# Hybrid decoder layer on one core: sums of weight blocks made by accumulating transfers, and the out-projection's operands fetched inside the last pair of products

## The chip, the cores and the metric

The kernel runs on one core of a Trainium2 chip. The metric is the device time of one execution in microseconds (us), from the runs of one measurement. The core's engines are PE (TensorE, matrix products), DVE (VectorE), ACT (ScalarE), POOL (GpSimd) and SP (SyncE, which here only issues transfers). "PEld" is PE's weight load, "PEclk" the clock that was granted to PE.

## The reference, cut to what matters

One layer (DEPTH = 1) of a decoder trunk, in float32, for 1024 positions of width 1024: an HGRN2 mixer with 8 heads of 128, then a squared-ReLU MLP.

```python
def _hgrn2_mixer(h, w_in, lower_bound, out_norm, w_out):
    proj = h @ w_in                              # 1024 x 4096
    q, f, i, g = jnp.split(proj, 4, axis=-1)
    ...                                          # log_f, k from f; qf = silu(q) / sqrt(128)
    o = _hgrn2_chunk_scan(heads(qf), heads(k), heads(i), heads(log_f))
    # S_t = diag(f_t) S_{t-1} + k_t v_t^T ; o_t = S_t^T q_t, for each head
    o = o * lax.rsqrt(jnp.mean(o * o, axis=-1, keepdims=True) + NORM_EPS)
    o = o.reshape(b, s, D_MODEL) * out_norm * jax.nn.silu(g)
    return o @ w_out

def reference(...):
    x = x + _hgrn2_mixer(_rmsnorm(x, norm_mix), ...)
    x = x + _squared_relu_mlp(_rmsnorm(x, norm_mlp), w1, w2)   # relu(h@w1)**2 @ w2
    return _rmsnorm(x, norm_final)
```

## The kernel before

**Products.** Each float32 operand is split in two parts of a shorter format: hi is a copy on ACT, lo the difference on DVE. A product is then three matmuls, hi·hi, hi·lo and lo·hi (`split_mm`, L208 to L210, 128x512 each).

**The projection h @ w_in** is cut into 16 pieces ("pairs", `pair`), n = 2h + j: for head h, j = 0 gives q and f, j = 1 gives v and g. The weights of piece n come as four blocks of 128x512, a, b, c, d: SP loads them in two transfers of 512 KB (`load_raw`, L144), a and c in one tile (named raw n 0), b and d in the other (raw n 1). The first two pieces are multiplied plainly. The other 14 use seven products of half-size blocks in place of eight, so they need sums of weight blocks: c+d is s1, a+c is s3, a+c+d is s2 and a+b+c+d is s4, each made in place in a raw block by DVE adds (`add`, L148), four adds for each n. `ensure` makes, in the order a, b, s1, s2, s3, s4, d, first the sums that a block needs and then its split (ACT at L168, DVE at L169) into one of eight slots m4 to m11, by the running number modulo 8. A slot is free again when PE has done the product eight jobs back. PE takes the blocks in the order a, b, s2, s1, s3, s4, d, twelve matmuls each; the blocks are asked for six jobs ahead.

**The scan.** Between a head's matmuls PE's stream has the scan units of an earlier head in it (`scan_units`), handed out one at a time by `pump` at a set spacing: small (L477), middle (L510, which needs qe, made by ACT at L499 and L503 and DVE at L504), leaf (L528), big (L558), kt (L573), vt (L584), kv (L596, which needs v, copied by ACT at L585), o, z and zt. The tables of level scores go by lv and Ac, the running products of the gates by f, q and k, and R and ht are sums of blocks of the normalised input and their splits.

**The output projection** (`proj_out`) multiplies z, the gated and normalised output of the scan, by w_out. z of heads 0 to 6 goes out to DRAM (zd, L641) and comes back in the layout wanted (iz, L700), w_out's blocks come by iw (L700), both are split (zh, wo: ACT at L689, DVE at L690) by `fetch`. In the program's text all fetches stand behind the last pair. The last head's scan units are pumped into the output projection. The MLP follows.

**Order of the work.** PE's order is the order of the text. At the start, up to the first two plain half pieces, ACT's, DVE's and POOL's are too. Behind that a planner sets the order on ACT, DVE, POOL and SP, by its own costs and the tiles' dependences; it may move a transfer or a split far ahead of where the text has it. Each engine then runs its list in that order, and waits at an instruction until its operands are ready.

Of the kernel before, what the change touches and what calls it, by code (L numbers as in the profile page):

```python
# [21 lines left out]
F32 = mybir.dt.float32  # L22
F32R = mybir.dt.float32r
U8 = mybir.dt.uint8
AF = mybir.ActivationFunctionType
ALU = mybir.AluOpType
# [3 lines left out]
P = 128  # L30
D = 1024
T = 1024
NH = 8
NC = T // P
# [14 lines left out]
def trunk(ctx: ExitStack, tc: tile.TileContext, x, gains, masks, gfin, w_in, w_out, w1, w2, out):  # L49
    nc = tc.nc  # L50
    pool = ctx.enter_context(tc.tile_pool(name="keep", bufs=1))
# [21 lines left out]
    def mslot(i, shape, name, dt=F32):  # L73
        return pool.tile(shape, dt, name=name, tag=f"m{i}")

    def hslot(half, kb, name):
        return pool.tile([P, 2, 512], F32R, name=name, tag=f"hT{half}{kb}")

    def dslot(i, shape, name, dt=F32):
        return dp.tile(shape, dt, name=name, tag=f"d{i}")  # L80
# [36 lines left out]
    def load_x(tb):  # L117
        nc.sync.dma_start(xs[tb], x[tb * P:(tb + 1) * P, :])
# [13 lines left out]
    PLAIN = 2  # L132
    ORDER = (("X", "a", "B11"), ("Z", "b", "B21"), ("X", "s2", "t2"), ("Y", "s1", "t1"),
             ("X", "s3", "t3"), ("Y", "s4", "B22"), ("X", "d", "t4"))
    jobs = [(n, m) for n in range(2 * NH) for m in ("abcd" if n < PLAIN else ("a", "b", "s1", "s2", "s3", "s4", "d"))]
    index = {j: i for i, j in enumerate(jobs)}
    raws = {}
    split = {}

    def load_raw(n):  # L140
        if n < 2 * NH:
            two = [mslot(2 * (n % 2) + i, [P, 2, 512], f"raw{n}{i}") for i in range(2)]
            for i in range(2):
                nc.sync.dma_start(two[i], w_in[n, i])  # L144
            raws[n] = {"a": two[0][:, 0], "c": two[0][:, 1], "b": two[1][:, 0], "d": two[1][:, 1]}

    def add(out_, a, b):
        nc.vector.tensor_tensor(out_, a, b, ALU.add)  # L148

    def ensure(count):  # L150

        while len(split) < min(count, len(jobs)):
            i = len(split)
            n, m = jobs[i]
            r = raws[n]
            if m == "s1":
                add(r["a"], r["a"], r["c"])
                add(r["c"], r["c"], r["d"])
            if m == "s2":
                add(r["c"], r["a"], r["d"])  # L160
            if m == "s4":
                add(r["c"], r["c"], r["b"])
            src = r[{"s1": "c", "s2": "c", "s4": "c", "s3": "a"}.get(m, m)]
            w = mslot(4 + i % 8, [P, 2, 512], f"w{n}{m}", F32R)
            step = P if i < 1 else 512
            for c in range(0, 512, step):
                o = slice(c, c + step)
                nc.scalar.activation(w[:, 0, o], src[:, o], AF.Copy)  # L168
                nc.vector.tensor_tensor(w[:, 1, o], src[:, o], w[:, 0, o].bitcast(F32), ALU.subtract)  # L169
            split[i] = w  # L170
            if m == "d":
                load_raw(n + 2)

# [71 lines left out]
    z_d = [dram.tile([P, T], F32, name=f"zd{h}") for h in range(NH - 1)]  # L245
    with tc.tile_pool(name="scan", bufs=1) as sp:
# [13 lines left out]
        lo = pool.tile([P, 8], F32, name="lbe")  # L260
# [105 lines left out]
        def f_bound(h, f):  # L366
            nc.vector.tensor_scalar(f, f, omlb[:, h:h + 1], lb[:, h:h + 1], op0=ALU.mult, op1=ALU.add)
# [38 lines left out]
        def pair(h, tl, j):  # L406

            n = 2 * h + j
            bank = {}
            for i, (b, m, src) in enumerate(ORDER):  # L410
                first = b not in bank
                if first:
                    bank[b] = psum.tile([P, 512], F32, name=f"p{b}{n}", tag="d")
                p_ = bank[b]
                w = weight(n, m)
                for kb in range(4):
                    c = slice(kb * P, (kb + 1) * P)
                    t = hc[src, kb]
                    split_mm(p_, w[:, 0, c], w[:, 1, c], t[:, 0], t[:, 1], first and kb == 0, kb == 3,
                             skip_group_check=True)  # L420
                    if kb == 1:
                        ensure(index[n, m] + AHEAD)
                    pump(650.0)
                if m in ("a", "s2", "s4", "b"):
                    name = "q" if j == 0 else "vT"
                    tiles(h, tl, name)
                    half = int(m in ("s2", "s4"))
                    dst = tl[name][:, HALF[half]]
                    if m in ("a", "s2"):
                        nc.scalar.activation(dst, p_, AF.Copy)  # L430
                    else:
                        add(dst, dst, p_)
                        if j == 0 and half:
                            q_part(h, tl, 0, tl["q"])
                elif m == "s1":
                    e = part(h, f"e{j}")
                    nc.scalar.activation(e, p_, AF.Copy)
                elif m == "s3":
                    add(e, e, p_)
                    (f_half, g_half)[j](h, tl, 1, e, -1.0)  # L440
                else:
                    (f_half, g_half)[j](h, tl, 0, p_, -1.0)
                    if j == 0:
                        f_bound(h, tl["f"])

        def prefixes(tl):

# [13 lines left out]
        def scan_units(h, tl):  # L461
# [60 lines left out]
            def leaf(m, i):  # L522
                def run():
                    ps = psum.tile([P, NC, LEAF], F32, name=f"lv{h}_{m}", tag="s")
                    for c in range(NC):
                        for b in range(P // LEAF):
                            s = slice(c * P + b * LEAF, c * P + (b + 1) * LEAF)
                            nc.tensor.matmul(ps[b * LEAF:(b + 1) * LEAF, c, :], k[:, s], q[:, s],  # L528
                                             start=True, stop=True)
                    carry(m)  # L530
                    nc.vector.copy_predicated(Ac, mk[:, i:i + 1, :].to_broadcast([P, NC, LEAF]), ps)  # L531
                    if m == LEAF // 2:
                        for b in range(P // LEAF):
                            r = slice(b * LEAF, (b + 1) * LEAF)
                            nc.scalar.activation(AT[r, :, r], Ac[r, :, :], AF.Copy)  # L535
                return run
# [93 lines left out]
            def zt():  # L630

                z = tl["sg"]
                for a in range(2):
# [7 lines left out]
                        nc.sync.dma_start(z_d[h][:, o], z[:, o])  # L641
                free("sg")

            return ([None] * (6 if h == 0 else 3) + [small, None, None] + [middle, None, leaf(16, 7)]
                    + [big(32), big(64), None, kt, ("values", h), vt, kv, None, o_unit, z_unit, None, zt])


        heads = {0: {}}
# [25 lines left out]
            pair(h, tl, 1)  # L674
            complete.add(("values", h))


        zh, wo = {}, {}
        items = [("z", half, h) for half in (0,) for h in range(NH - 1)] + [("w", 0, h) for h in range(NH)]
        items += [("z", 1, h) for h in range(NH - 1)] + [("w", 1, h) for h in range(NH)]  # L680
        item_no = [0]

        def place(what, half, h):
            if what == "z":
                return hslot(half, (h, (h + 4) % 8)[half], f"zh{half}{h}")
            return dslot((h, (8, 9, 10, 11, 0, 1, 2, 3)[h])[half], [P, 2, 512], f"wo{half}{h}", F32R)

        def split_value(t, src):
            nc.scalar.activation(t[:, 0], src, AF.Copy)  # L689
            nc.vector.tensor_tensor(t[:, 1], src, t[:, 0].bitcast(F32), ALU.subtract)  # L690

        def fetch(what, half, lo, hi):

            for h0 in range(lo, hi, 2):
                raw = mslot(item_no[0] % 4, [P, 2, 512], f"i{what}{half}{h0}")
                item_no[0] += 1
                for i in range(min(2, hi - h0)):
                    h = h0 + i
                    src = z_d[h][:, HALF[half]] if what == "z" else w_out[h * P:(h + 1) * P, HALF[half]]
                    nc.sync.dma_start(raw[:, i], src)  # L700
                for i in range(min(2, hi - h0)):
                    h = h0 + i
                    t = (zh if what == "z" else wo)[half, h] = place(what, half, h)
                    split_value(t, raw[:, i])

        xs = [mslot(4 + tb, [P, D], f"xr{tb}") for tb in range(NC)]

        def proj_out(tbs, dh, hs, after=None):

# [11 lines left out]

        o0 = slice(0, 512)
        A, B = range(NC // 2), range(NC // 2, NC)
        last = NH - 1
        fetch("z", 0, 0, last)
        fetch("w", 0, 0, last)
        for tb in range(NC):
            load_x(tb)
        proj_out(A, 0, range(last))
        fetch("z", 1, 0, last)  # L730
        fetch("w", 0, last, NH)
        proj_out(B, 0, range(last))
        fetch("w", 1, 0, 4)
        drain_units()
        for half in range(2):
            t = zh[half, last] = place("z", half, last)
            split_value(t, heads[last]["sg"][:, HALF[half]])
        proj_out(A, 0, (last,))
        proj_out(B, 0, (last,))
        fetch("w", 1, 4, NH)  # L740


    SEQ = (("X", "a", "B11"), ("Y", "s1", "t1"), ("X", "s2", "t2"), ("Y", "s4", "B22"),
# [11 lines left out]
    raw = {}  # L755
# [389 lines left out]
```

## Time and profile before

| | us |
|---|---|
| time, median of 3 runs | 1171.9 (1171.43 to 1175.21) |
| the profiled execution's own time | 1173.07 |
| its span | 1171.2 |
| PE busy | 1145.7 (98%) |
| DVE busy | 796.5 (68%) |
| ACT busy | 569.1 (49%) |
| POOL busy | 68.5 (6%) |
| mean granted clock of PE | 0.991 |

The rows below read as follows. A row of the timeline gives the start in us, the duration, the engine, the line of the kernel, the operation, output<-input, the shape and how many such instructions stand in a row; in square brackets how long the engine was idle just before, and what ended that. Names such as w8s stand for the split of an s block of piece 8, raw for a raw block. A row with a stretch (100.00:425.00) sums all engines over it. "SPq" is SP's queue of transfers.

### The profile page before, as it was taken

How to read it: one execution, taken by the hardware profiler on the slowest of the kernel's cores; microseconds unless marked ns; L12 is line 12 of the kernel's file. 1: busy time of each engine (PE TensorE's matmuls, PEld its weight loads, DVE VectorE, ACT ScalarE, POOL GpSimd, SP SyncE). 2: the span in 40 equal slices, each digit the busy share in tenths (PEclk: the TensorE clock that was granted, in tenths of full speed). 3: DMA queues.
4: the chain of work that ended last, by engine and by line, in shares of the span. 5: the costliest groups of instructions: out<-in, count | busy, mean ns of one | idle time of the engine just before them, and what ended most of it. 6: DMA issues, size and time to landing. Idle time of an engine off the chain costs nothing.

```text
span 1171.2 us, 17554 instructions
## 1 busy us (share of the span) xinstructions
PE 1145.7 (98%) x7108; PEld 948.1 (81%) x7108; DVE 796.5 (68%) x1131; ACT 569.1 (49%) x999; POOL 68.5 (6%) x94
## 2 busy tenths in 40 slices
PE   8989999999999998999999999999999999999997
PEld 7777788887878786888888888888888888888886
DVE  5897878787787867524856545654578756677673
ACT  7546465564745554236635445545453443323552
POOL 6500000000000000011000000000000000000011
PEclk9999999999999998999999999999999999999999
DMA  6111112111111176112244244523798554432331
GB/s 257 37 37 37 55 55 60 50 55 55 37 55 62 48 216 195 40 72 91 90 162 165 93 156 180 197 100 117 277 347 309 180 180 155 155 104 91 126 126 72
DMA packets 43138, 143.38 MB, mean 122 GB/s; under 512 B 4912, under 2 KB 5040, under 8 KB 43056
## 3 DMA queue, kind: packets, MB, share of 16 engines
q1 hardware_dynamic: 42192, 141.05, 34.1%
q8 instruction: 56, 0.92, 0.3%
q10 hardware_dynamic: 864, 1.20, 0.3%
q14 instruction: 26, 0.21, 0.1%
HBM read 100.81 MB, written 41.42 MB: 121 GB/s over the span
## 4 chain that ended last, share of the span: by engine, by line
PE 85%; DVE 8%; DMA 2%; ACT 2%; POOL 1%; issue 1%; SPq 0%; POOLq 0%; DVEq 0%; ACTq 0%
PE m2X L210 5%; PE m2X L209 5%; PE m2X L208 5%; PE m1X L208 4%; PE m1X L209 4%; PE m1X L210 4%; PE pX L208 3%; PE pX L210 3%; PE pX L209 3%; PE op L208 3%; PE m2Y L210 2%; PE m2Y L209 2%; PE m2Y L208 2%; PE op L210 2%; PE op L209 2%; PE m1Y L208 2%
## 5 line engine op out<-in xcount | busy, mean ns | idle before, releaser
L946 ACT ACTIVATE a<-ai 128x1024 fp32r<-128x1024 f32 x56 | 59.0, 1053 | 71.4 <-PE m2X L209 23.5
L947 DVE TENSOR_TENSOR a<-ai,a 128x1024 fp32r<-128x1024 f32 x56 | 68.3, 1219 | 11.3 <-ACT a L946 11.3
L849 ACT ACTIVATE e<-e 128x1024 f32<-128x1024 f32 x21 | 22.3, 1062 | 67.3 <-DVE e L980 67.3
L208 PE MATMUL op<-wo,zh 128*128 128x512 f32 x128 | 51.8, 405 | 0.0
L210 PE MATMUL op<-wo,zh 128*128 128x512 f32 x128 | 50.7, 396 | 0.0
L209 PE MATMUL op<-wo,zh 128*128 128x512 f32 x128 | 50.6, 395 | 0.0
L148 DVE TENSOR_TENSOR xr<-xr,op 128x512 f32<-128x512 f32 x24 | 16.4, 687 | 44.6 <-PE op L210 44.5
L1007 DVE TENSOR_TENSOR acc<-acc,m2X 128x512 f32<-128x512 f32 x32 | 21.1, 684 | 36.1 <-PE m2X L210 36.0
L322 DVE TENSOR_TENSOR q<-q,f 128x512 f32<-128x512 f32 x56 | 38.5, 688 | 3.7 <-PE lv L558 2.1
L329 DVE TENSOR_TENSOR k<-k,f 128x512 f32<-128x512 f32 x56 | 38.3, 685 | 0.2 <-PE lv L510 0.2
L122 POOL TENSOR_SCALAR rs_f<-fs 128x1 f32<-128x1 f32 x4 | 2.1, 513 | 577.7 <-ACT ot L1011 577.7
L846 ACT ACTIVATE e<-e 128x1024 f32<-128x1024 f32 x32 | 34.0, 1062 | 1.0
L535 ACT ACTIVATE AT<-Ac 32x256 f32<-32x256 f32 x32 | 13.3, 415 | 33.9 <-DVE Ac L531 33.6
L148 DVE TENSOR_TENSOR raw<-raw,raw 128x512 f32<-128x512 f32 x42 | 28.9, 689 | 0.7
L210 PEld LDWEIGHTS op<-wo,zh 128*128 128x128 f32 x128 | 24.4, 191 | 5.4
L208 PEld LDWEIGHTS op<-wo,zh 128*128 128x128 f32 x128 | 24.6, 192 | 5.1
L209 PEld LDWEIGHTS op<-wo,zh 128*128 128x128 f32 x128 | 24.6, 192 | 4.9
L968 ACT ACTIVATE e<-m1X 128x512 f32<-128x512 f32 x28 | 16.0, 592 | 19.9 <-PE m1X L210 19.9
L301 POOL TENSOR_TENSOR R<-h0B 128x512 f32<-128x512 f32 x16 | 25.3, 1610 | 6.0 <-DVE h0B L298 6.0
L122 POOL TENSOR_SCALAR rs_z<-zs 128x8 f32<-128x8 f32 x8 | 1.9, 242 | 401.2 <-ACT z L621 401.2
L627 ACT ACTIVATE z<-o,rs_z 128x128 f32<-128x128 f32 x64 | 17.4, 383 | 16.4 <-POOL rs_z L123 16.4
L615 PE MATMUL o<-v,AT 128*128 128x128 f32 x128 | 23.4, 275 | 0.0
(1720 smaller groups left out, 3753.8 us busy)
## 6 DMA issues: line engine op xcount, KB each, us to landing
raw<-in_w_in SPq DMA_DIRECT2D x32, 512.0 KB, 3.6
ai<-adt SPq DMA_DIRECT2D x32, 512.0 KB, 4.4
adB<-e SPq DMA_DIRECT2D x24, 512.0 KB, 2.6
adt<-t SPq DMA_DIRECT2D x24, 512.0 KB, 4.3
ai<-adB SPq DMA_DIRECT2D x24, 512.0 KB, 4.5
x<-in_x SPq DMA_DIRECT2D x8, 512.0 KB, 7.3
xr<-in_x SPq DMA_DIRECT2D x8, 512.0 KB, 5.5
iw<-in_w_out SPq DMA_DIRECT2D x16, 256.0 KB, 3.8
```

The lines of the kernel that those rows point to most:

```text
L148: nc.vector.tensor_tensor(out_, a, b, ALU.add)
L208: nc.tensor.matmul(ps, lhi, rhi, start=start, stop=False, **more)
L209: nc.tensor.matmul(ps, lhi, rlo, start=False, stop=False, **more)
L210: nc.tensor.matmul(ps, llo, rhi, start=False, stop=stop, **more)
L301: nc.gpsimd.tensor_tensor(R[half, kb // 2][:, kb % 2], t[:, 0].bitcast(F32), t[:, 1].bitcast(F32), ALU.add)
L322: nc.vector.tensor_tensor(qo, qo, te.to_broadcast([P, n, m]), ALU.mult)
L329: nc.vector.tensor_tensor(ke, ke, to.to_broadcast([P, n, m]), ALU.mult)
L615: nc.tensor.matmul(ps[:, j, :], AT[:, c, :], v[:, c, :], start=True, stop=c == 0)
L846: nc.scalar.activation(t, t, AF.Square)
L849: nc.scalar.activation(t, t, AF.Relu, scale=sign)
L946: nc.scalar.activation(hi, x, AF.Copy)
L947: nc.vector.tensor_tensor(lo, x, hi.bitcast(F32), ALU.subtract)
```

## The change

- Accumulating transfers: the 56 adds of weight blocks on DVE go. Instead `more` has POOL's queue issue a transfer from w_in in DRAM that is added to a raw block as it lands (256 KB each): c gets d right after the load; after the split of a, a gets c; after the split of s1, c gets a; after the split of s2, c gets b.
- The slots of the splits are permuted (`PLACES`).
- Fetches for the output projection are written inside the last pair, behind the products b, s2, s1 and s3 (`LEFT`): z of heads 0 to 5, then w_out of heads 0 to 3, of 4 to 6, then z of head 6, into other slots than before; x is loaded again at the head of the output projection.
- `scan_units` has the small unit one step earlier, with one more step between it and middle.

```diff
+    PLACES = (6, 7, 8, 9, 10, 4, 11, 5)
+    CHAIN = {"a": ("a", "c"), "s1": ("c", "a"), "s2": ("c", "b")}
...
             raws[n] = {"a": two[0][:, 0], "c": two[0][:, 1], "b": two[1][:, 0], "d": two[1][:, 1]}
+            if n >= PLAIN:
+                more(n, "c", "d")
+
+    def more(n, m, other):
+        i, k = {"a": (0, 0), "c": (0, 1), "b": (1, 0), "d": (1, 1)}[other]
+        nc.gpsimd.dma_start(raws[n][m], w_in[n, i, :, k], accum_op=ALU.add)
...
-            if m == "s1":
-                add(r["a"], r["a"], r["c"])
-                add(r["c"], r["c"], r["d"])
-            if m == "s2":
-                add(r["c"], r["a"], r["d"])
-            if m == "s4":
-                add(r["c"], r["c"], r["b"])
             src = r[{"s1": "c", "s2": "c", "s4": "c", "s3": "a"}.get(m, m)]
-            w = mslot(4 + i % 8, [P, 2, 512], f"w{n}{m}", F32R)
+            w = mslot(PLACES[i % 8], [P, 2, 512], f"w{n}{m}", F32R)
...
             split[i] = w
+            if n >= PLAIN and m in CHAIN:
+                more(n, *CHAIN[m])
...
+                if (h, j) == (last, 1) and m in LEFT:
+                    fetch(*LEFT[m])
...
-            return ([None] * (6 if h == 0 else 3) + [small, None, None] + [middle, None, leaf(16, 7)]
+            return ([None] * (5 if h == 0 else 2) + [small, None, None, None] + [middle, None, leaf(16, 7)]
...
+    LEFT = {"b": ("z", 0, range(last - 1), ("m0", "m1", "m8")), "s2": ("w", 0, range(4), ("hT07", "m9")),
+            "s1": ("w", 0, range(4, last), ("m10", "m11")), "s3": ("z", 0, range(last - 1, last), ("m0",))}
...
         xs = [mslot(4 + tb, [P, D], f"xr{tb}") for tb in range(NC)]
+        for tb in range(NC):
+            load_x(tb)
...
-        fetch("z", 0, 0, last)
-        fetch("w", 0, 0, last)
-        for tb in range(NC):
-            load_x(tb)
         proj_out(A, 0, range(last))
-        fetch("z", 1, 0, last)
-        fetch("w", 0, last, NH)
+        fetch("z", 1, range(last), ("m2", "m3", "m0", "m1"))
+        fetch("w", 0, range(last, NH), ("m2",))
```

The line numbers move by some 3 to 7 in this part of the kernel (L168 becomes L171, L148 L158, L301 L306, L503 L510, L689 and L690 L664 and L665).

POOL at the start, first before, then now: the statistics of the last rows of x (rs_n), then the end of the sums R. raw20 is the tile with the blocks a and c of piece 2.

```order
L122 TENSOR_SCALAR rs_n5_335<-ss5_333 128x1
L123 TENSOR_TENSOR rs_n5_335<-rs_n5_335,neghalf_75 128x1
L122 TENSOR_SCALAR rs_n6_350<-ss6_348 128x1
L123 TENSOR_TENSOR rs_n6_350<-rs_n6_350,neghalf_75 128x1
L122 TENSOR_SCALAR rs_n7_363<-ss7_361 128x1
```

```order
L122 TENSOR_SCALAR rs_n5_335<-ss5_333 128x1
L123 TENSOR_TENSOR rs_n5_335<-rs_n5_335,neghalf_75 128x1
L155 DMA raw20_344<-in_w_in 128x512
L122 TENSOR_SCALAR rs_n6_351<-ss6_349 128x1
L123 TENSOR_TENSOR rs_n6_351<-rs_n6_351,neghalf_75 128x1
L122 TENSOR_SCALAR rs_n7_364<-ss7_362 128x1
```

The transfer into c of piece 2 now stands between the statistics of rows 5 and 6; that of piece 3 stands in the same way between the last two adds of R (L306).

ACT in the steady stretch, in piece 8, before and now; w8s1 to w8s4 and w8d are splits, qe3 the middle unit's operand of head 3.

```order
L168 ACTIVATE w8s2_2322<-raw80_1935 128x512
L168 ACTIVATE w8s4_2410<-raw80_1935 128x512
L374 ACTIVATE sig13_2312<-e13_2291 128x512
L168 ACTIVATE w8d_2469<-raw81_1936 128x512
L499 ACTIVATE qe3_2367<-q3_1923 128x32x16
L374 ACTIVATE sig03_2399<-pX7_2167 128x512
L168 ACTIVATE w9a_2530<-raw90_2226 128x512
L503 ACTIVATE qe3_2367<-q3_1923 128x32x16
```

```order
L171 ACTIVATE w8s2_2375<-raw80_1936 128x512
L379 ACTIVATE sig13_2366<-e13_2294 128x512
L171 ACTIVATE w8s4_2411<-raw80_1936 128x512
L506 ACTIVATE qe3_2351<-q3_1924 128x32x16
L171 ACTIVATE w8d_2470<-raw81_1937 128x512
L510 ACTIVATE qe3_2351<-q3_1924 128x32x16
```

The split of s4 moved behind sig13 and stands right ahead of the first qe copy; the split of piece 9's a moved behind the second.

DVE in the output projection's first part, before and now; zh06 is the split of head 6's z, k7, f7 and q7 lead to the middle unit of head 7.

```order
L148 TENSOR_TENSOR e17_4425<-e17_4425,pX15_4311 128x512
L378 TENSOR_TENSOR sg7_4440<-sig17_4441,e17_4425 128x512
L690 TENSOR_TENSOR zh06_4561<-iz06_4559,zh06_4561 128x512
L488 COPY_PREDICATED Ac_177<-mk_74,lv7_0_0_4453 128x128
L489 COPY_PREDICATED Ac_177<-mk_74,lv7_0_0_4453 128x64
L329 TENSOR_TENSOR k7_4234<-k7_4234,f7_4235 128x512
```

```order
L158 TENSOR_TENSOR e17_4470<-e17_4470,pX15_4312 128x512
L665 TENSOR_TENSOR zh10_4845<-iz10_4842,zh10_4845 128x512
L383 TENSOR_TENSOR sg7_4499<-sig17_4500,e17_4470 128x512
L334 TENSOR_TENSOR k7_4235<-k7_4235,f7_4236 128x512
L665 TENSOR_TENSOR zh06_4505<-iz06_4503,zh06_4505 128x512
L340 TENSOR_TENSOR f7_4236<-f7_4236 128x512
L495 COPY_PREDICATED Ac_177<-mk_74,lv7_0_0_4511 128x128
```

The first k product moved ahead of the subtract of zh06, and a subtract of the second half (zh10) in front of both.

More of the change, by code (lines that the diff above doesn't have):

```diff
@@ L642, in zt, with place, split_value, fetch @@
                 free("sg")
-            return ([None] * (6 if h == 0 else 3) + [small, None, None] + [middle, None, leaf(16, 7)]
+            return ([None] * (5 if h == 0 else 2) + [small, None, None, None] + [middle, None, leaf(16, 7)]
                     + [big(32), big(64), None, kt, ("values", h), vt, kv, None, o_unit, z_unit, None, zt])
+        zh, wo = {}, {}
+        last = NH - 1
+        def place(what, half, h):
+            if what == "z":
+                return hslot(half, (h, (h + 4) % 8)[half], f"zh{half}{h}")
+            return dslot(((h + 4) % 8, (8, 9, 10, 11, 4, 5, 6, 7)[h])[half], [P, 2, 512], f"wo{half}{h}", F32R)
+        def split_value(t, src):
+            nc.scalar.activation(t[:, 0], src, AF.Copy)
+            nc.vector.tensor_tensor(t[:, 1], src, t[:, 0].bitcast(F32), ALU.subtract)
+        def fetch(what, half, heads_, places):
+            for h0, m in zip(heads_[::2], places):
+                raw = pool.tile([P, 2, 512], F32, name=f"i{what}{half}{h0}", tag=m)
+                two = range(h0, min(h0 + 2, heads_[-1] + 1))
+                for h in two:
+                    src = z_d[h][:, HALF[half]] if what == "z" else w_out[h * P:(h + 1) * P, HALF[half]]
+                    nc.sync.dma_start(raw[:, h - h0], src)
+                for h in two:
+                    t = (zh if what == "z" else wo)[half, h] = place(what, half, h)
+                    split_value(t, raw[:, h - h0])
+        LEFT = {"b": ("z", 0, range(last - 1), ("m0", "m1", "m8")), "s2": ("w", 0, range(4), ("hT07", "m9")),
+                "s1": ("w", 0, range(4, last), ("m10", "m11")), "s3": ("z", 0, range(last - 1, last), ("m0",))}
         heads = {0: {}}
@@ L675, in trunk @@
             complete.add(("values", h))
[L678 to L704, printed above, removed]
         xs = [mslot(4 + tb, [P, D], f"xr{tb}") for tb in range(NC)]
+        for tb in range(NC):
+            load_x(tb)
         def proj_out(tbs, dh, hs, after=None):
@@ L723, in trunk @@
         A, B = range(NC // 2), range(NC // 2, NC)
-        last = NH - 1
-        fetch("z", 0, 0, last)
-        fetch("w", 0, 0, last)
-        for tb in range(NC):
-            load_x(tb)
         proj_out(A, 0, range(last))
-        fetch("z", 1, 0, last)
-        fetch("w", 0, last, NH)
+        fetch("z", 1, range(last), ("m2", "m3", "m0", "m1"))
+        fetch("w", 0, range(last, NH), ("m2",))
         proj_out(B, 0, range(last))
-        fetch("w", 1, 0, 4)
+        fetch("w", 1, range(4), ("m3", "m0"))
         drain_units()
@@ L739, in trunk @@
         proj_out(B, 0, (last,))
-        fetch("w", 1, 4, NH)
+        fetch("w", 1, range(4, NH), ("m1", "m2"))
     SEQ = (("X", "a", "B11"), ("Y", "s1", "t1"), ("X", "s2", "t2"), ("Y", "s4", "B22"),
```

## The prediction

> **What bounds the kernel now.** I read the page first (busy shares, chain), then the span cut into stretches, then each place where the matrix engine (PE) stands still, then the queues that release it.
>
> ```profile
> PE 1145.7 (98%) x7108; PEld 948.1 (81%) x7108; DVE 796.5 (68%) x1131; ACT 569.1 (49%) x999; POOL 68.5 (6%) x94
> PE 85%; DVE 8%; DMA 2%; ACT 2%; POOL 1%; issue 1%; SPq 0%; POOLq 0%; DVEq 0%; ACTq 0%
> 75.00:100.00 25.00, 20.09 (x252) 15.59 (x250) 20.77 (x46) 11.82 (x26) 0.00 (x0) 0.93 0.13 43
> 100.00:425.00 325.00, 323.05 (x2961) 267.63 (x2960) 256.75 (x487) 179.77 (x456) 13.38 (x14) 1.00 0.19 60
> 425.00:450.00 25.00, 19.72 (x194) 15.77 (x193) 17.30 (x38) 11.13 (x19) 0.00 (x0) 0.86 0.77 241
> 450.00:475.00 25.00, 25.00 (x235) 20.59 (x234) 15.76 (x32) 8.39 (x19) 0.00 (x0) 1.00 0.48 159
> ```
>
> The first row gives busy times, the second the shares of the chain. A stretch has its length, then PE, its weight loads, DVE, ACT and POOL, then the granted clock, the DMA engines' share and GB/s. PE is the bound: 98% of the span, 85% of the chain. From 100 to 425 us, where nearly all of the seven-product pairs run, it idles 325 − 323.05 = 1.95 us in all, although DVE is 79% busy. Work taken from DVE there can win those 1.95 us and no more. What else can be won stands in the two stretches with a low PE share and clock, 75 to 100 us and 425 to 450 us:
>
> ```profile
> 80.57 1.30 PE L510 MATMUL lv<-qe,k 128*32 128x48 f32 x64 [3.02 <-DVE qe L504]
> 95.67 0.96 PE L573 MATMUL kt<-ident,k 128*128 128x128 f32 x7 [1.89 <-DVE tot L545]
> 443.88 1.51 PE L510 MATMUL lv<-qe,k 128*32 128x48 f32 x64 [5.28 <-ACT qe L503]
> 445.32 0.80 PE L208 MATMUL op<-wo,zh 128*128 128x512 f32 x1
> 449.88 0.39 PE L210 MATMUL op<-wo,zh 128*128 128x512 f32 x1
> 450.11 0.39 PE L208 MATMUL op<-wo,zh 128*128 128x512 f32 x1
> ```
>
> Square brackets hold the idle time and its releaser. At 443.88 PE has waited 5.28 us, since 438.6. Behind that wait it is slow: eleven matmuls start between 445.32 and 449.88, 4.56 us, where eleven at the pitch of 0.23 (449.88 to 450.11) are 2.5; and L510 itself takes 1.51 against 0.89 in a steady pair (233.05, further down). That is 2.06 + 0.62 = 2.7 us lost to the lowered clock, 8.0 us in all for this stall.
>
> **The change part by part.** (1) 56 DVE adds go, four in each of 14 pairs. In their place stand 56 transfers of 256 KB issued on POOL, each behind the split that last read the block, and the next split waits for the landing.
>
> ```profile
> L148 DVE TENSOR_TENSOR raw<-raw,raw 128x512 f32<-128x512 f32 x42 | 28.9, 689 | 0.7
> L148 DVE TENSOR_TENSOR raw<-raw 128x512 f32<-128x512 f32 x14 | 9.6, 689 | 0.2
> raw<-in_w_in SPq DMA_DIRECT2D x32, 512.0 KB, 3.6
> iz<-zd SPq DMA_DIRECT2D x6, 256.0 KB, 2.9
> DMA to landing us min/median/max: 2.5/3.9/7.5
> L144 SPq DMA_DIRECT2D raw<-in_w_in x32: 327/328/738, 2.6 to 355.8; - x32
> 30.24 0.78 POOL L122 TENSOR_SCALAR rs_n<-ss 128x1 f32<-128x1 f32 x1
> 38.31 11.32 POOL L301 TENSOR_TENSOR R<-h0B 128x512 f32<-128x512 f32 x6 [0.75 <-DVE h0B L298]
> ```
>
> 28.9 + 9.6 = 38.5 us of DVE. No row of this trace has an accumulating transfer, or any issued by POOL. Let L be the time from the end of a split to the landing of the block behind it, with POOL's issue time I in it. Lower bounds: I = 0.33 (SP's issue) and L = 0.33 + 2.9 (the quiet 256 KB read before 430 us) = 3.2. Upper: I = 1.9 (a POOL add, 11.32 over 6) and L = 1.9 + 7.5 (the longest landing of the out-projection's loads, in the row with min, median and max) = 9.4. I take I = 0.8, POOL's small operation (0.78), since it too is mostly a fixed cost, and 3.6 for the landing: the w_in row is the same source and stretch, and its twice as many bytes stand for a block that is read and written again. L = 4.4.
>
> An even pair in the steady stretch (n = 8), then an odd one (n = 9):
>
> ```profile
> 218.32 0.69 DVE L169 TENSOR_TENSOR w8s<-raw,w8s 128x512 fp32r<-128x512 f32 x1 [2.51 <-ACT w8s L168]
> 221.98 0.62 ACT L168 ACTIVATE w8s<-raw 128x512 fp32r<-128x512 f32 x1
> 232.19 0.62 ACT L503 ACTIVATE qe<-q 128x512 f32<-128x512 f32 x1
> 233.05 0.89 PE L510 MATMUL lv<-qe,k 128*32 128x48 f32 x64
> 246.20 0.60 ACT L437 ACTIVATE e<-pY 128x512 f32<-128x512 f32 x1
> 252.72 1.07 ACT L585 ACTIVATE v<-vt 128x512 f32<-128x512 f32 x2
> 254.94 1.27 PE L596 MATMUL kv<-v,kt 128*128 128x128 f32 x10
> ```
>
> Even: the split of s1 ends at 219.0. Then a transfer (L), the split of s2 (copy and subtract, 0.7 + 0.7), a second transfer (L), and the copy of s4. In ACT's new order that copy stands ahead of both qe copies, which PE's middle unit (L510) awaits: four ACT operations of 0.6. PE could start L510 at 219.0 + 1.4 + 2.4 + 2L = 222.8 + 2L and gets there at 233.05: free while L is up to 5.1. Odd: the copy of s2 follows that of e, at 246.7, its split ends at 248.1, then one transfer, the copies of s4 and d (0.53 each, the pitch of ACT's copies) and v's (1.07): kv could start at 250.2 + L, PE gets there at 254.94: free up to 4.7. At 4.4 both hold, with 1.4 and 0.3 us to spare. So the transfers cost 0 here, hidden by PE's own products, and as DVE's load falls the small stalls go: −1.9. Once the cover is gone the cost is 2·6·(L − 5.1) over six even pairs and 7·(L − 4.7) over seven odd ones, 19 us for each us of L.
>
> (2) The start. Two issues now stand in POOL's queue ahead of work that PE awaits, one between the row statistics, one before the last add of R:
>
> ```profile
> 31.10 0.57 POOL L123 TENSOR_TENSOR rs_n<-rs_n,neghalf 128x1 f32<-128x1 f32 x1
> 31.70 0.75 DVE L189 TENSOR_SCALAR x<-x,rs_n 128x1024 f32<-128x1024 f32 x1 [0.76 <-POOL rs_n L123]
> 32.51 0.33 PE L196 MATMUL tr<-ident,x 128*128 128x128 f32 x1 [1.19 <-DVE x L189]
> 34.43 1.28 POOL L301 TENSOR_TENSOR R<-h0B 128x512 f32<-128x512 f32 x1 [2.76 <-DVE h0B L298]
> 49.66 1.23 DVE L97 TENSOR_TENSOR R<-R,R 128x1024 f32<-128x1024 f32 x1 [1.18 <-POOL R L301]
> 66.03 0.68 DVE L169 TENSOR_TENSOR w2b<-raw,w2b 128x512 fp32r<-128x512 f32 x1
> ```
>
> DVE waits for POOL at 31.70 and PE for DVE at 32.51, so the first I goes through; the second goes through to 49.66. From there DVE sets the end up to L510 at 80.57. Three adds ahead of it go (−2.1) and a product for sg moves behind it (−0.6): by DVE alone L510 would come 2.7 − 2I = 1.1 us sooner. But pair 2 has the same ladder with no slack: its s1 can be split by 66.03 + 0.68 + 0.6 = 67.3, then L, 1.4, L, and on ACT s4, sig, w3a, qe, q, qe (six of some 0.53, 3.3 with the step to PE): 72.0 + 2I + 2L = 82.4, 1.8 later than 80.57. Of the stall at 95.67 (1.89, for DVE) I take half as given back, 0.9, as DVE has less to do. Net +0.9; bounds −1.5 (I = 0.33, L = 3.2, the ladder at 79.1) and +3.1 (I = 1.9).
>
> (3) The last pair. The fetches are now written inside it, but the planner had already put several of them there:
>
> ```profile
> 378.95 26.51 SPq L700 DMA_DIRECT2D iz<-zd  x6
> 425.19 0.86 SPq L641 DMA_DIRECT2D zd<-sg  x2
> 431.61 0.32 SPq L700 DMA_DIRECT2D iz<-zd  x1
> 435.92 0.63 ACT L689 ACTIVATE zh<-iz 128x512 fp32r<-128x512 f32 x1 [4.22 <-DMA iz<-zd]
> 436.59 0.69 DVE L690 TENSOR_TENSOR zh<-iz,zh 128x512 fp32r<-128x512 f32 x1 [3.58 <-ACT zh L689]
> 442.00 0.68 DVE L504 TENSOR_TENSOR qe<-q,f 128x512 f32<-128x512 f32 x1
> 443.21 0.62 ACT L503 ACTIVATE qe<-q 128x512 f32<-128x512 f32 x1
> ```
>
> So the 5.28 us are a round trip: head 6's z goes out at 425.19, SP reads it back 6.4 us later, 4.3 more until ACT has it, and the operations up to qe stand behind DVE's subtract. In the new order this subtract still stands ahead of that chain, with the first k product now in front of it; SP has one x load ahead of the write where it had weights and x. I let the write land after 4.8 us, between the quiet 2.9 and the 6.4, at 430.0; the read at 434.3 (4.3 as before); copy and subtract end at 435.6 (1.3) instead of 437.28. From there to the end of qe on DVE (442.68) were 5.4 us for 14 operations; now 10 of these stand there, without that k product (0.6) and three Ac copies (some 0.2 each, the rest of the 5.4 behind seven products of 0.6): 4.2, so L510 could start at 439.8. PE is there at 438.6: a stall of 1.2, and behind one of 1.89 (95.67) the next op takes no longer. So 1.2 − 5.28 − 2.7 = −6.8. Bounds: −2.4, if the round trip is as long as before and only what stands between the subtract and L510 shrinks, from 6.6 to 4.2; −8.0, if the stall goes whole.
>
> (4) The slot permutation moves no work: 0. The small unit one step sooner puts it ahead of six matmuls, 1.4 us, between which PE has no wait: 0. From 450 us on PE is full (25.00 of 25) and what follows is the same: 0.
>
> Sum: +0.9 − 1.9 − 6.8 = −7.8. The profiled execution took 1173.07 (span 1171.2 and 1.9 around it), so 1165.3 by its own time; it stands 1.2 over the median of the runs, 1171.9, from which 1164.1 follows.
>
> The Trainium skill, page "DMA: Bandwidth & Descriptors", section "Anatomy of one DMA — SWDGE (gpsimd) path", fits a transfer issued by GpSimd with 2.0 us plus its bytes over 436e3 per us: an estimate of 2.6 us here, below my low bound; by it the start would be −1.1, the sum −9.8 and the time 1162.1. No run before the change shows such a transfer.
>
> **The rivals.** R1, slower: the transfers are late. Start and last pair are −5.9 at L = 4.4; the start adds 2 per us of L, the steady stretch 19. It breaks even where 12(L − 5.1) + 7(L − 4.7) + 2(L − 4.4) = 5.9, at L = 5.2, and at L = 6 the time is 17.2 longer, 1189.1. For it: the median landing of 3.9 and an issue of 1.9 make 5.8, and whatever stands behind a late split on ACT and DVE is late too. Against it: the DMA engines are 19% busy in that stretch, and 512 KB land in 3.6.
>
> The Trainium skill, page "SBUF — State Buffer", section "Who interferes with whom", says that a transfer issued by GpSimd can be held up while DVE runs a copy or tensor_scalar in a mode that takes the port pair shared with GpSimd. By it L grows beside such operations, which is R1. POOL's add of 1.28 (34.43) against 1.9 each (38.31) is the nearest that the trace shows.
>
> R2, small gain: the round trip of head 6 stays as long, −2.4 instead of −6.8: 1168.5. For it: z is written no sooner, and the read still waits for it. Against: the queue ahead of it is shorter.
>
> R3: an issue costs POOL 1.9 at the start, +3.1 instead of +0.9: 1166.3. For it: POOL's adds take that long; against: its small operations take 0.57 and 0.78.
>
> **How the numbers follow.** Forecast 0.52 (1164.1, its own range 1160 to 1168), R1 0.25, R2 0.13, R3 0.10. A difference under 0.3%, 3.5 us, can't be told from none, so faster is below 1168.4: 0.50 of the forecast, half of R2 and most of R3, 0.63. The same is the rest of R2, some of the others, and R1 up to L = 5.35: 0.13. Slower: 0.24. The range goes from 1160 (the transfers near the lower bound) to 1180, which is R1 at L = 5.6; beyond that lie some 0.17, below 1160 some 0.03.
>
> **What would show it.** DVE's busy time falls by some 38 us and POOL has 56 transfers. Between 100 and 425 us PE idles under 1 us if L is under 4.7; if L510 and kv show waits for ACT in every pair, the prediction is wrong by tens of us. The start is right if head 0's L510 begins near 82.4, the last pair if its L510 waits 1 to 2 us with matmuls 0.23 apart behind it. R2 shows as a wait of 4 us there, R3 as a tr matmul that comes 2 us later than 32.51.

## The result, and the profile after

| kernel | median, us | runs | against before, 95% interval |
|---|---|---|---|
| before | 1171.93 | 5 | |
| changed | 1183.97 | 5 | 1.0104 [1.0084, 1.0124] |
| before, second measurement | 1172.75 | 7 | |
| changed, second measurement | 1182.32 | 4 | 1.0086 [1.0071, 1.0101] |

The change makes the kernel about 1% slower, 10 to 12 us; 1164.1 was predicted, and 1180 was the top of the range. The profile read here is that of the second measurement (span 1180.6), since the first one's fell in a run of 2951 us at less than half of PE's pace, such as the kernel before had once too (2952).

The page's first row, then the stretches to 100, 425 and 500 us: of before only the two that weren't shown, then of the changed kernel. Length, PE, its weight loads, DVE, ACT, POOL, granted clock, DMA share, GB/s.

```profile
0.00:100.00 100.00, 88.73 (x644) 73.14 (x644) 77.97 (x130) 57.66 (x106) 37.52 (x42) 0.95 0.27 97
425.00:500.00 75.00, 69.72 (x549) 57.44 (x548) 46.65 (x89) 27.77 (x68) 1.91 (x2) 0.95 0.44 141
```

```profile
PE 1142.6 (97%) x7108; PEld 944.3 (80%) x7108; DVE 758.5 (64%) x1075; ACT 568.9 (48%) x999; POOL 118.4 (10%) x150
0.00:100.00 100.00, 85.03 (x629) 69.11 (x630) 74.23 (x122) 56.04 (x104) 44.27 (x51) 0.97 0.43 120
100.00:425.00 325.00, 312.61 (x2895) 258.02 (x2894) 213.33 (x422) 170.71 (x422) 53.05 (x59) 1.00 0.41 91
425.00:500.00 75.00, 71.64 (x587) 59.76 (x586) 48.26 (x94) 37.52 (x104) 3.82 (x4) 1.00 0.49 164
```

DVE's busy time falls by 38.0 us, as forecast. Between 100 and 425 us PE now idles 325 − 312.61 = 12.39 us where it was 1.95: +10.4. Up to 100 us it idles 14.97 instead of 11.27. Behind 425 us it idles 3.36 instead of 5.28, and the clock stays at full: the last pair did gain. What PE waits for between 100 and 425 us (releaser, sum of the waits in us, how many, the longest):

```profile
PE lv L535 <- DVE k L334: 5.8, 6, 1.1
PE lv L517 <- DVE qe L511: 3.6, 4, 1.4
PE lv L565 <- DVE k L334: 2.8, 6, 1.0
PE lv L565 <- DVE f L340: 0.2, 1, 0.2
```

All of it is in the even pairs (six in this stretch), most at the leaf unit (L535), not at the middle unit's qe (L517), and none at kv. One transfer and one pair, n = 8: the group of all transfers, then in order of time DVE's subtract for s1, POOL's issue, ACT's copy and DVE's subtract for s2, the copies for s4 and qe, the last gate products, and PE.

```profile
L155 POOL DMA_DIRECT2D raw<-in_w_in x56: 856/870/1172, 28.6 to 415.3; - x56
DMA to landing us min/median/max: 3.6/4.4/6.0
224.84 0.69 DVE L172 TENSOR_TENSOR w8s<-raw,w8s 128x512 fp32r<-128x512 f32 x1 [2.72 <-ACT w8s L171]
225.94 0.94 POOL L155 DMA_DIRECT2D raw<-in_w_in  x1 [3.86 <-DVE w8s L172]
230.80 0.63 ACT L171 ACTIVATE w8s<-raw 128x512 fp32r<-128x512 f32 x1 [2.41 <-DMA raw<-in_w_in]
231.47 0.69 DVE L172 TENSOR_TENSOR w8s<-raw,w8s 128x512 fp32r<-128x512 f32 x1 [4.01 <-ACT w8s L171]
236.60 0.63 ACT L171 ACTIVATE w8s<-raw 128x512 fp32r<-128x512 f32 x1 [3.18 <-DMA raw<-in_w_in]
237.14 0.62 ACT L506 ACTIVATE qe<-q 128x512 f32<-128x512 f32 x1
237.79 0.69 DVE L327 TENSOR_TENSOR q<-q,f 128x512 f32<-128x512 f32 x1
238.53 0.69 DVE L511 TENSOR_TENSOR qe<-q,f 128x512 f32<-128x512 f32 x1
239.36 0.89 PE L517 MATMUL lv<-qe,k 128*32 128x48 f32 x64
244.17 0.69 DVE L334 TENSOR_TENSOR k<-k,f 128x512 f32<-128x512 f32 x1
245.01 0.75 PE L535 MATMUL lv<-q,k 128*32 128x32 f32 x64 [1.09 <-DVE k L334]
```

The split of s1 ends at 225.53, the block of s2 is there at 230.80: L = 5.3 (0.4 until POOL issues, 4.9 to the landing). DVE stands idle for 4.01 us and then works with hardly a gap until PE's leaf unit is fed: from 232.16, where s2's subtract ends, it is 7.1 us to the end of qe and 12.7 to the end of the k product that leaf needs. The gate products are those of before, pushed into less time.

### The profile page after: what moved, and what is told of

It reads as the page before. It is cut to its first block, busy times and chain, and to the rows that moved or that the text cites. A ratio compares the mean times of both kernels' runs of the same rounds, so it can differ in the third digit from the quotient of the medians.

```text
span 2949.6 us, 17681 instructions
## 1 busy us (share of the span) xinstructions
PE 2941.0 (100%) x7108; PEld 1795.3 (61%) x7108; DVE 773.4 (26%) x1075; ACT 580.5 (20%) x999; POOL 113.7 (4%) x150
## 3 DMA queue, kind: packets, MB, share of 16 engines
q1 hardware_dynamic: 42192, 141.05, 13.5%
## 4 chain that ended last, share of the span: by engine, by line
PE 100%; DVE 0%; ACT 0%; POOL 0%; POOLq 0%; issue 0%
PE m2X L214 5%; PE m2X L213 5%; PE m2X L215 5%; PE pX L213 5%; PE m1X L214 5%; PE m1X L213 5%; PE pX L214 5%; PE m1X L215 5%; PE pX L215 4%; PE op L213 3%; PE m2Y L215 3%; PE m2Y L213 3%; PE op L214 3%; PE m2Y L214 3%; PE op L215 3%; PE pY L213 2%
## 5 line engine op out<-in xcount | busy, mean ns | idle before, releaser
L213 PE MATMUL op<-wo,zh 128*128 128x512 f32 x128 | 107.6, 841 | 0.0
L214 PE MATMUL op<-wo,zh 128*128 128x512 f32 x128 | 105.7, 826 | 0.0
L215 PE MATMUL op<-wo,zh 128*128 128x512 f32 x128 | 105.5, 824 | 0.0
L155 POOL DMA_DIRECT2D raw<-in_w_in x56 | 49.4, 882 | 709.6 <-DMA raw<-in_w_in 79.1
L853 ACT ACTIVATE e<-e 128x1024 f32<-128x1024 f32 x21 | 22.3, 1060 | 250.0 <-DVE e L984 250.0
L158 DVE TENSOR_TENSOR xr<-xr,op 128x512 f32<-128x512 f32 x24 | 16.5, 689 | 182.0 <-PE op L215 182.0
L215 PEld LDWEIGHTS op<-wo,zh 128*128 128x128 f32 x128 | 44.6, 348 | 31.1 <-issue 30.7
L213 PEld LDWEIGHTS op<-wo,zh 128*128 128x128 f32 x128 | 44.2, 345 | 30.2 <-issue 28.2
L214 PEld LDWEIGHTS op<-wo,zh 128*128 128x128 f32 x128 | 45.4, 355 | 28.1 <-issue 28.1
L622 PE MATMUL o<-v,AT 128*128 128x128 f32 x128 | 51.1, 535 | 0.0
L1011 DVE TENSOR_TENSOR acc<-acc,m2Y 128x512 f32<-128x512 f32 x16 | 11.0, 689 | 146.7 <-PE m2Y L215 146.7
L622 PEld LDWEIGHTS o<-v,AT 128*128 128x128 f32 x128 | 46.6, 432 | 3.7 <-issue 3.7
L624 PE MATMUL o<-S,q 128*128 128x128 f32 x112 | 47.0, 539 | 0.0
L624 PEld LDWEIGHTS o<-S,q 128*128 128x128 f32 x112 | 41.9, 441 | 0.0
L603 PEld LDWEIGHTS kv<-v,kt 128*128 128x128 f32 x112 | 35.4, 432 | 3.5 <-issue 3.5
```

The costliest lines, as they stand in the source:

```text
L155: nc.gpsimd.dma_start(raws[n][m], w_in[n, i, :, k], accum_op=ALU.add)
L213: nc.tensor.matmul(ps, lhi, rhi, start=start, stop=False, **more)
L214: nc.tensor.matmul(ps, lhi, rlo, start=False, stop=False, **more)
L215: nc.tensor.matmul(ps, llo, rhi, start=False, stop=stop, **more)
L603: nc.tensor.matmul(ps[:, j, :], st["kt"][:, c, :], v[:, c, :], start=True, stop=True)
L622: nc.tensor.matmul(ps[:, j, :], AT[:, c, :], v[:, c, :], start=True, stop=c == 0)
```

## The experiments

Each is the changed kernel or the one before with one edit; the kernel before was measured beside them each time, at 1172.75 for the first three rows, 1172.32 for the next four and 1172.11 for the last four.

| kernel | transfers | median, us | against before, 95% interval |
|---|---|---|---|
| all but the transfers | 0 | 1164.87 | 0.9934 [0.9919, 0.9949] |
| transfers alone | 56 | 1219.43 | 1.0404 [1.0381, 1.0426] |
| changed, transfers from piece 4 on | 48 | 1179.95 | 1.0060 [1.0045, 1.0075] |
| changed, early sums alone by transfer | 28 | 1168.82 | 0.9972 [0.9960, 0.9984] |
| changed, late sums alone by transfer | 28 | 1195.03 | 1.0189 [1.0172, 1.0206] |
| changed, early sums from piece 4 on | 24 | 1165.54 | 0.9945 [0.9932, 0.9958] |
| transfers and the earlier small unit | 56 | 1188.84 | 1.0137 [1.0121, 1.0153] |
| changed, s2's sum on DVE | 42 | 1171.77 | 0.9993 [0.9982, 1.0004] |
| changed, s4's sum on DVE | 42 | 1182.24 | 1.0087 [1.0070, 1.0104] |
| changed, s2's subtract on POOL | 56 | 1192.26 | 1.0171 [1.0151, 1.0192] |
| earlier small unit alone | 0 | 1170.05 | 0.9981 [0.9972, 0.9990] |

**Which stretch, which part.** First the changed kernel again, unedited.

> The changed kernel once more, for a profile to be read beside that of before. Three theories for the 12 us that it is slower by. T1, late transfers: the ladder of accumulating transfers holds PE in the steady stretch; then PE idles 10 to 20 us between 100 and 425 us (1.95 before), in waits of 0.5 to 1.5 us released by ACT at L517 or kv, in nearly every pair. T2, the start: the two issues on POOL and pair 2's ladder; then 10 us or more of new idle time lies before 100 us and the steady stretch stays full. T3, the last pair: the fetches collide there; then the new idle time lies behind 415 us.

The stretches above bear out T1 as to the place; but the waits are released by DVE, not by ACT, and stand in the even pairs alone. Then all but the transfers:

```diff
             if n >= PLAIN:
-                more(n, "c", "d")
...
+            if m == "s1":
+                add(r["a"], r["a"], r["c"])
+                add(r["c"], r["c"], r["d"])
+            if m == "s2":
+                add(r["c"], r["a"], r["d"])
+            if m == "s4":
+                add(r["c"], r["c"], r["b"])
...
-            if n >= PLAIN and m in CHAIN:
-                more(n, *CHAIN[m])
```

> All of the change but the accumulating transfers: the sums of weight blocks are DVE adds as before; the slots, the fetches inside the last pair and the earlier small unit are as changed. T1 and T2: faster than before by the 6.8 us forecast for the last pair or part of it, 1164 to 1169 us. T3: slower than before, about 1180.

1164.87. Its stretches, and PE at the last pair's middle unit:

```profile
0.00:100.00 100.00, 88.36 (x646) 72.04 (x647) 78.74 (x131) 58.17 (x108) 37.83 (x42) 0.97 0.28 97
100.00:425.00 325.00, 324.26 (x2968) 269.01 (x2967) 256.46 (x491) 183.27 (x461) 13.40 (x14) 1.00 0.20 62
425.00:500.00 75.00, 72.87 (x573) 60.15 (x572) 44.00 (x85) 24.88 (x64) 2.72 (x4) 1.00 0.39 136
436.73 0.89 PE L525 MATMUL lv<-qe,k 128*32 128x48 f32 x64 [0.78 <-DVE qe L519]
```

The stall of 5.28 us has become 0.78, and the clock stays up; PE idles 2.13 us in the last stretch, as leaf and big of the last head now wait 1.01 and 0.34. With all 56 adds back on DVE, PE idles 0.74 us between 100 and 425 us. T3 is out, and so the transfers cost 1182.3 − 1164.9 = 17.4 us. The transfers alone, in the kernel before (`more` and `CHAIN` as in the change):

```diff
+            if n >= PLAIN:
+                more(n, "c", "d")
...
-            if m == "s1":
-                add(r["a"], r["a"], r["c"])
-                add(r["c"], r["c"], r["d"])
-            if m == "s2":
-                add(r["c"], r["a"], r["d"])
-            if m == "s4":
-                add(r["c"], r["c"], r["b"])
...
+            if n >= PLAIN and m in CHAIN:
+                more(n, *CHAIN[m])
```

> The kernel before with the accumulating transfers in place of the DVE adds and nothing else. T1 and T2: slower than before by the 12 us of the whole change plus what the last pair wins, 1186 to 1192. T3: no slower than before, 1168 to 1173.

1219.43: here the transfers cost 46.7 us, in the changed kernel 17.4. T3 had it at no cost; T1 and T2 had it 27 us too low. The largest sum of PE's waits in it (from 60 to 500 us), then DVE's subtract for s4 and PE's middle unit of piece 8's time:

```profile
PE lv L513 <- DVE qe L507: 34.7, 7, 5.7
249.05 0.69 DVE L170 TENSOR_TENSOR w8s<-raw,w8s 128x512 fp32r<-128x512 f32 x1 [3.38 <-ACT w8s L169]
255.63 1.51 PE L513 MATMUL lv<-qe,k 128*32 128x48 f32 x64 [4.57 <-DVE qe L507]
```

Here the planner put the subtract of s4 too ahead of the gate products in DVE's queue, so they wait for two landings. Behind its wait of 4.57 us L513 takes 1.51 instead of 0.89, and the granted clock from 250 to 262 us is 0.72. Then the start, with pieces 2 and 3 summed on DVE (its adds stand there for n < 4, as above):

```diff
-            if n >= PLAIN:
+            if n >= 4:
                 more(n, "c", "d")
...
-            if n >= PLAIN and m in CHAIN:
+            if n >= 4 and m in CHAIN:
                 more(n, *CHAIN[m])
```

> The changed kernel with the sums of pieces 2 and 3 on DVE as before, so that no accumulating transfer is left at the start (48 of 56 stay). T1: 1180 to 1183, a gain of 1 to 3 us from the two pieces. T2: most of the loss goes, 1165 to 1172. T3: 1182 to 1184.

1179.95, at the lower edge of T1's range and 2.4 less than 1182.32: the start costs that much. T2 is out.

**Which sums, and through which queue.** Early sums (c gets d, a gets c) against late ones:

```diff
-    CHAIN = {"a": ("a", "c"), "s1": ("c", "a"), "s2": ("c", "b")}
+    CHAIN = {"a": ("a", "c")}
...
+            if m == "s2":
+                add(r["c"], r["a"], r["d"])
+            if m == "s4":
+                add(r["c"], r["c"], r["b"])
```

> The changed kernel with only the two early sums of each piece by transfer (c gets d after the load, a gets c after the split of a); the sums for s2 and s4 are DVE adds as before. Theory Q, the queue: what costs time is that the block of s2 lands some 5.3 us after the split of s1 and DVE's subtract of it stands ahead of the gate products up to qe and leaf. Then PE idles under 2 us between 100 and 425 us, and the time is that of the kernel without transfers, 1164.9, plus 1 to 3 us at the start: 1166 to 1168. Theory P, the price of any transfer on POOL (DVE or ACT slowed beside it, or the DMA engines): half of the 17.4 us between 1182.3 and 1164.9 stays, 1172 to 1175.

1168.82, 0.8 above Q's range and 3 below P's. Its steady stretch:

```profile
100.00:425.00 325.00, 324.22 (x2971) 269.13 (x2970) 241.08 (x463) 183.19 (x459) 33.78 (x37) 1.00 0.31 78
```

PE idles 0.78 us beside 28 transfers. The other way round:

```diff
-    CHAIN = {"a": ("a", "c"), "s1": ("c", "a"), "s2": ("c", "b")}
+    CHAIN = {"s1": ("c", "a"), "s2": ("c", "b")}
...
-                more(n, "c", "d")
...
+            if m == "s1":
+                add(r["a"], r["a"], r["c"])
+                add(r["c"], r["c"], r["d"])
```

> The changed kernel with only the two late sums of each piece by transfer (c gets a after the split of s1, c gets b after the split of s2); the first two sums are DVE adds as before. Q: the loss stays, 1178 to 1184, with waits at L517's place and at leaf in nearly every even pair. P: half of it stays, 1172 to 1175.

1195.0. P falls, as the same number of transfers now costs all of the loss and more; but the time is 11 above Q's range. Three of PE's waits (60 to 500 us), then ACT's copies for s4 and for v, and PE's kv, in piece 7:

```profile
PE lv L536 <- DVE k L335: 10.5, 7, 1.8
PE lv L518 <- ACT qe L511: 5.0, 1, 5.0
PE kv L604 <- ACT v L593: 4.9, 2, 2.5
213.79 0.63 ACT L172 ACTIVATE w7s<-raw 128x512 fp32r<-128x512 f32 x1 [2.78 <-DMA raw<-in_w_in]
214.84 1.06 ACT L593 ACTIVATE v<-vt 128x512 f32<-128x512 f32 x2
215.47 2.31 PE L604 MATMUL kv<-v,kt 128*128 128x128 f32 x14 [2.51 <-ACT v L593]
```

The leaf waits are longer, up to 1.8, with the early adds back on DVE; why, I did not follow. Two waits at kv and one for ACT at the middle unit are new. The waits at kv are the path that the prediction named for odd pairs: v's copy stands on ACT behind the copies for s4 and d, and the copy for s4 waits for its landing. The wait of 5.0 is head 0's middle unit, at the start, where ACT's qe copy stands behind piece 2's copy for s4 in the same way.

> As the one with the early sums by transfer, but from piece 4 on; pieces 2 and 3 have all four sums on DVE, so no transfer of POOL is left at the start. Q: what the start costs goes too, 1163 to 1166, against 1164.9 for the kernel without any such transfer. P: 1171 to 1174.

The edit is that for the early sums, with n >= 4 and with all four adds on DVE for pieces 2 and 3. 1165.54: the start's cost goes, and what is left is the time of the kernel without any accumulating transfer. Taking 24 adds off DVE wins nothing.

> The kernel before with the accumulating transfers, and with the small unit one step earlier; the fetches and the slots are as before. With the transfers alone DVE's subtract of s4 stands ahead of the gate products, so that two landings hold up qe; with the small unit earlier it stands behind qe, and one landing does. Q: 1182.3 plus the 6.8 to 7.9 of the last pair, 1188 to 1192, instead of 1219.4. P: no less than 1215, as the transfers are the same 56.

```diff
-            return ([None] * (6 if h == 0 else 3) + [small, None, None] + [middle, None, leaf(16, 7)]
+            return ([None] * (5 if h == 0 else 2) + [small, None, None, None] + [middle, None, leaf(16, 7)]
```

1188.84, within Q's range: one unit moved by one step takes 30.6 us off the kernel with transfers alone, since it makes the planner put s4's subtract behind qe. The same step in the kernel before, by itself:

> The kernel before with the small unit one step earlier and nothing else, to part the win of 7.9 us of all but the transfers. If the win is the fetches in the last pair, as the prediction has it: 1170 to 1172. If the earlier unit makes it, by letting the planner put the gate products earlier: 1165 to 1168.

1170.05, a win of 2.1 of the 7.9 us; the rest is the fetches, with the slots. Its steady stretch:

```profile
100.00:425.00 325.00, 324.29 (x2967) 268.81 (x2966) 254.80 (x488) 180.67 (x456) 13.38 (x14) 1.00 0.20 61
```

With all 56 adds on DVE PE idles 0.71 us there, where it idled 1.95.

**Which of the two late landings.** One of the two late sums back on DVE, with the edit for s2 (that for s4 is alike):

```diff
-    CHAIN = {"a": ("a", "c"), "s1": ("c", "a"), "s2": ("c", "b")}
+    CHAIN = {"a": ("a", "c"), "s2": ("c", "b")}
+            if m == "s2":
+                add(r["c"], r["a"], r["d"])
```

> The changed kernel with the sum for s2 alone back on DVE (42 transfers stay). If the landing of s2's block is the one that counts, because its subtract stands ahead of the gate products in DVE's queue (theory Q2), the steady stretch is nearly full again: 1167 to 1171 us. If it is the landing of s4's block, whose copy stands ahead of both qe copies on ACT, as the prediction had it (theory Q4), the loss stays: 1178 to 1183.

> The changed kernel with the sum for s4 alone back on DVE (42 transfers stay). Q2: the loss stays and grows a little, since the add and the subtract of s4 now stand on DVE ahead of the gate products too: 1182 to 1192. Q4: the loss goes, 1167 to 1171.

1171.77 and 1182.24: Q2 for both, the first 0.8 above its range. The steady stretch with s2's sum on DVE:

```profile
100.00:425.00 325.00, 323.50 (x2964) 267.71 (x2963) 229.19 (x448) 179.75 (x452) 44.74 (x49) 1.00 0.37 86
```

14 transfers fewer, and 11 of the 12.4 us of idle time are gone; 14 fewer at s4 change nothing. More than half of the 6.9 us that are left over 1164.87 lies at the start: up to 100 us PE is busy 84.64 us, against 88.36 without any transfer. Last, s2's subtract on POOL:

```diff
-                nc.vector.tensor_tensor(w[:, 1, o], src[:, o], w[:, 0, o].bitcast(F32), ALU.subtract)
+                low = nc.gpsimd if m == "s2" else nc.vector
+                low.tensor_tensor(w[:, 1, o], src[:, o], w[:, 0, o].bitcast(F32), ALU.subtract)
```

> The changed kernel with all 56 transfers, but the subtract of s2's split done by POOL, so that no instruction in DVE's queue waits for the block of s2. The landings are as late as before. Q2: most of the loss of the steady stretch goes, although POOL's subtract takes 1.3 to 1.9 us instead of 0.69 and s4 comes that much later: 1169 to 1176. Q4: s4's block comes later still, 1184 or more.

1192.26, what Q4 gave and not Q2. POOL's subtract, ACT's copy for s4, and DVE behind it, in piece 8:

```profile
235.59 1.29 POOL L173 TENSOR_TENSOR w8s<-raw,w8s 128x512 fp32r<-128x512 f32 x1 [4.88 <-ACT w8s L171]
241.29 0.63 ACT L171 ACTIVATE w8s<-raw 128x512 fp32r<-128x512 f32 x1 [5.27 <-DMA raw<-in_w_in]
242.48 0.69 DVE L328 TENSOR_TENSOR q<-q,f 128x512 f32<-128x512 f32 x1 [1.45 <-ACT qe L507]
```

DVE no longer waits for s2, but a q product waits for ACT's qe copy, which stands behind the copy of s4, which waits for the second landing, later by POOL's slower subtract. So both ways exist, and in the changed kernel they lie close together: there the same q product began at 237.79, right behind the qe copy (237.14 + 0.62) that follows the copy of s4 at 236.60. The landing of s2 comes first and shifts both; taking it out frees both, taking only DVE's way or only s4's landing away does not. What ACT's way costs by itself this run does not show, since it also makes the second landing later.

## Why the prediction was wrong, point by point

**The steady stretch: forecast −1.9, measured +10.4. This step failed.** Two things went wrong in "the transfers cost 0 here, hidden by PE's own products". The landing was put at L = 4.4 and is 5.3 in piece 8: the median from issue to landing is 4.4 by itself, 4.9 in this case, and 0.4 passes from the end of the split to POOL's issue. And I followed ACT's queue alone, to qe, and not DVE's. With the rows of before, and with DVE's order and its 12.7 us as the changed kernel's trace has them, the step would have run: s1's split ends at 219.0, L, the split of s2 1.4, then 12.7 us of DVE work to the k product that leaf awaits, 0.15 to PE: 233.2 + L. Before, leaf began at

```profile
237.49 0.76 PE L528 MATMUL lv<-q,k 128*32 128x32 f32 x64
```

without a wait, so the cover held up to L = 4.2, not 5.1, and at 5.3 leaf waits 1.1; measured 1.09. That order is: s2's subtract, then the gate products, then s4's, d's and the next a's splits ahead of the k product of leaf. R1's formula gives 6.6 us for this stretch at L = 5.3, of which 4.2 in odd pairs, where PE waited for nothing; the even pairs alone idle 12.4. R1 was the right rival, with the wrong place in the even pairs and too low a price.

**DVE's load, −1.9, and the small unit, 0.** The early sums alone take 28 adds away and PE idles 0.78 us; but with none taken away and the small unit earlier, the one edit, it idles 0.71. So 1.2 of the 1.95 us go with the order of units and need no relief of DVE, and the term put at 0, since PE has no wait there, won 2.1 us in all. What less load alone would win, with the small unit where it was, no run shows.

**The start: forecast L510 of head 0 at 82.4 and +0.9 net.** DVE's subtract for s1 of piece 2, the one for s2, ACT's copy for s4, and PE:

```profile
66.99 0.69 DVE L172 TENSOR_TENSOR w2s<-raw,w2s 128x512 fp32r<-128x512 f32 x1
73.41 0.68 DVE L172 TENSOR_TENSOR w2s<-raw,w2s 128x512 fp32r<-128x512 f32 x1
78.72 0.63 ACT L171 ACTIVATE w2s<-raw 128x512 fp32r<-128x512 f32 x1 [4.55 <-DMA raw<-in_w_in]
82.47 0.89 PE L517 MATMUL lv<-qe,k 128*32 128x48 f32 x64 [3.52 <-DVE qe L511]
97.98 0.95 PE L580 MATMUL kt<-ident,k 128*128 128x128 f32 x7 [1.63 <-DVE k L334]
```

The path of the ladder was right, its sum to 0.1 us by luck: the two issues were to shift the split of s1 from 67.3 by 1.6, and it ends at 67.7; the 1.2 us too many made up for terms that were each too short. What was to be given back was not: of the 1.89 us at kt 1.63 are left, the small unit waits 0.98 anew, kt starts 2.3 us later than at 95.67, and with pieces 2 and 3 on DVE the time falls by 2.4. R3's price of 1.9 for an issue isn't what it takes: 1.09 and 0.95 for the two at the start, 0.87 in the median. Two of the prediction's bounds here don't follow from its own terms. L has I in it, so I = 1.9 makes L = 5.5 and the ladder 86.8: +5.3 and not +3.1. And the 0.9 given back is in the forecast and the upper bound, but not in the lower one (−1.5), nor in the −1.1 that an L of 2.6 was to give.

**The last pair: forecast −6.8, a stall of 1.2 and no fall of the clock.** With all but the transfers it is a stall of 0.78, no fall, and a time 7.9 us below before, of which the small unit has some 2.1. This step held, less the 1.3 us that leaf and big now wait, and R2 did not: head 6's z is read back 4.25 us after it goes out (422.47 to 426.72), where 4.8 were forecast and it was 6.4. In the changed kernel 2.01 us are left at the same place, and the round trip is again what PE waits for, 4.7 us and then 4.8 until ACT has it:

```profile
438.86 0.98 SPq L648 DMA_DIRECT2D zd<-sg  x2
443.57 0.32 SPq L674 DMA_DIRECT2D iz<-zd  x1
449.01 0.69 DVE L665 TENSOR_TENSOR zh<-iz,zh 128x512 fp32r<-128x512 f32 x1 [3.31 <-ACT zh L664]
454.06 0.89 PE L517 MATMUL lv<-qe,k 128*32 128x48 f32 x64 [2.01 <-DVE qe L511]
```

**The price of a landing.** By the fit in the Trainium skill, page "DMA: Bandwidth & Descriptors", section "Anatomy of one DMA — SWDGE (gpsimd) path", L was estimated at 2.6. An accumulating transfer of 256 KB takes 4.4 us (3.6 at the least) from issue to landing here, so the fit doesn't serve as a price for one. The Trainium skill, page "SBUF — State Buffer", section "Who interferes with whom", has it that DVE can hold up a transfer issued by GpSimd while it runs in a mode that takes the port pair shared with GpSimd. That doesn't show in POOL's issues, which last 0.86 to 1.17 us over all 56; why one landing takes 3.6 us and another 6.0, no run here tells.

**The sum.** The start of one and the same matmul in both kernels gives the account: the first of the output projection, then one behind the last head's big unit, first before, then changed.

```profile
435.71 0.39 PE L208 MATMUL op<-wo,zh 128*128 128x512 f32 x1
457.95 0.39 PE L208 MATMUL op<-wo,zh 128*128 128x512 f32 x1
449.17 0.39 PE L213 MATMUL op<-wo,zh 128*128 128x512 f32 x1
467.04 0.39 PE L213 MATMUL op<-wo,zh 128*128 128x512 f32 x1
```

The changed kernel is 2.3 us behind at head 0's kt, 13.5 at the first of these, 9.1 at the second, and 9.4 at the end of the span (9.6 by the medians). So the start costs 2.3 us, the steady stretch 11.2, of which 10.4 are idle time, the last pair wins 4.4, and 0.3 is lost behind it. No kernel here beats the one without accumulating transfers, 1164.87.

## What to carry to other kernels

Moving work from a busy engine to transfers pays only if the engine's load sets the end; where the work stands between dependent steps, it lengthens their chain by a landing each, and an engine that runs its list in order then waits with all that stands behind. So price such a change by the first instruction in each queue that awaits the landing, followed through everything behind it to PE, on every queue and not only on the one that looked critical. In this kernel the sums that are made long before they are needed went to transfers for free (1165.54 against 1164.87, from piece 4 on); the sum for s2, between two splits, did not.

## What the runs showed of the hardware

```profile
q1 hardware_dynamic: 42192, 141.05, 33.2%
q0 software_dynamic: 8064, 14.68, 8.2%
```

In the changed kernel (queue, packets, MB, share of the time of 16 DMA engines; q0 has the accumulating transfers, q1 the plain ones) the accumulating transfers take 0.56% of the engines' time for each MB, the plain ones 0.24%: 2.4 times as much. That is seen in the steady stretch, where the DMA share rises from 0.19 to 0.41. An issue by POOL is 0.87 us, against 0.33 by SP.
